# Turning keys by VectorE in 32x32 squares instead of by TensorE, in a two-layer encoder step

## The chip, the cores and the metric

The kernel runs on one core of one Trainium2 chip. The metric is the device time of one execution in microseconds; lower is better. TensorE (PE) multiplies, VectorE (DVE), ScalarE (ACT) and GpSimd (POOL) work on elements, SyncE (SP) issues nearly all DMA transfers, ACT issues a few, and sixteen DMA engines carry them out.

## The reference

A streaming encoder step with two groups, a prompt of 2048 frames and a sample of 64 frames that follow 2048 cached ones. Layer a is attention over a band of chunks, layer b is stick-breaking attention over all earlier frames. 16 heads of 64, width 1024, all in float32. Besides the two results it returns the new keys and values:

```python
qp, kp, vp, gp = a_project(xp, norm_a[i], w_in_a[i])        # layer a: rms_norm, then one product
op = chunk_band_prompt(qp, kp, vp, rel_bias_a[i])
k_all = jnp.concatenate([cache_a_k[i], ks], axis=1)         # 512 cached rows, then 64 new ones
o_s = band_attend(qs, k_all, v_all, q_pos_s, k_pos_a, rel_bias_a[i])
xp = xp + gated_out(op, gp, w_out_a[i])
...
kb_p, vb_p = shared_kv(xp, norm_kv, w_kv)                   # layer b
kb_all = jnp.concatenate([cache_b_k, kb_s], axis=1)         # 2048 cached rows, then 64 new ones
op = sb_prompt(qp, kb_p, vb_p)
o_s = sb_block(qs, kb_all, vb_all, q_pos_s, k_pos_b)
...
return (y_prompt, y_sample, new_a_k_prompt, new_a_v_prompt, kb_p, vb_p,
        new_a_k_sample, new_a_v_sample, kb_s, vb_s)
```

Keys enter as rows of one frame (`cache_a_k`, `cache_b_k`: frames x 1024) and leave as rows of one frame (`new_a_k_prompt`: the last 512 frames of the prompt, `kb_p`: all 2048, and the two of the sample). Inside, the kernel keeps keys with the features on the partitions and the frames along the row. So keys are turned on the way in and on the way out.

## The kernel before

The program goes through four stages: projections of layer a (to about 656 us in the profile), band attention of layer a (to about 1300 us), projections of layer b (to about 2030 us) and stick-breaking attention of layer b. Products are made in split form: each operand is held as a high and a low part, and three products are added.

`projections` first makes the values, then runs jobs: for layer a the kinds k, q, g, for layer b k, g, q, each over eight pairs of heads (`hp`). A job loads 128 columns of weights (`wraw`, on ACT's DMA queue), splits them, multiplies them with the turned inputs (`x_own` for the first 1088 frames, `big` for the other 1024) into banks of PSUM (`ps_t`, five buffers), and empties each bank: ACT copies the high part (`sh`), DVE subtracts for the low part (`sl`); `g` jobs have one part, `sg`. These tiles have five buffers and are stored to scratch memory by SP. For some kinds (`DEFER`) the second half is left for later jobs that run beside the attention. Of layer a's keys the second half is such a job; of layer b's keys nothing is.

Between the jobs stand pieces of staging, shared out evenly by program order. Those that the change touches, or that it stands beside:

- `stage_cache` (from L430) takes 512 cached frames of one pair of heads: it loads `kr` (L434, 512 rows of 512 bytes, one buffer), turns it by four PE transposes into the PSUM bank `ps_c`, splits that into `kh` and `kl` and stores both. Layer a has 8 such pieces, layer b 32, of which 8 are staged in layer a's projections and 24 in layer b's.
- `stage_diff` (`vcur`, `vprev`) makes differences of values, and `stage_w_out` (`vcur` from `w_out_b`, stored to `wo`) splits the last weights; they have no turns, but share queues and buffers.
- `natural` (from L509) writes keys' rows for the outputs: `kf` is the sum of high and low part (made by POOL), four PE transposes turn it into the bank `ps_n`, ACT copies it to `kn` (two buffers), and one DMA stores it (L515). In layer b it runs for four blocks of 512 frames of each pair, in both layers for the 64 frames of the sample.
- `token_rows`, in the late jobs, does the same for the last 512 frames of layer a's prompt: `lkn` into `ps_r`, a copy by ACT, a store through `queue`.

The banks `ps_c`, `ps_n` and `ps_r` come from one pool of three (`bank`, tag `wt`), which other transposes and late jobs use too.

Each engine and each DMA queue works in order. Within the projections the order is set by a scheduler that simulates the program; within the attention stages instructions keep program order, except some loads and stores. At the end of layer b's projections stand `LEAD["b"] = 14` steps of late jobs on PE (six products of 512 columns each) before the first scores; the first loads of the attention (`q`, `kt`, `vt`) come behind `gf`, the last norm's weights, on SP's queue.

```python
def flip(out, in_):
    pe.transpose(out, in_, ident[: in_.shape[0], : in_.shape[0]])
...
staged += [partial(stage_diff, "cache", t, i) for t in range(PAST // P) for i in range(2)]
keys_b = [partial(stage_cache, "b", hp, c) for hp in range(HP) for c in range(PAST // CH)]
staged += keys_b[:8]
```

Of the kernel before, what the change touches and what calls it, by code (L numbers as in the profile page):

```python
# [9 lines left out]
F32 = mybir.dt.float32  # L10
F32R = mybir.dt.float32r
AF = mybir.ActivationFunctionType
# [4 lines left out]
P = 128  # L17
# [15 lines left out]
CH = 512  # L33
# [32 lines left out]
def place(r):  # L66
    h, c = spot(r)
    return HALVES[h][0] + c


def f32(ap):
    return ap.bitcast(F32)
# [28 lines left out]
def encoder_step(ctx: ExitStack, tc: tile.TileContext, a: dict, o: dict):  # L101
    nc = tc.nc
    order = InOrder(tc)
    dve, act, gps, pe = (order.engine(x) for x in (nc.vector, nc.scalar, nc.gpsimd, nc.tensor))
    mm = pe.matmul

    def in_place(what):


        def pinned():  # L110
            was, order.on = order.on, order.amid
            what()
            order.on = was

        return pinned
# [23 lines left out]
    queue = Queue(24)  # L139
# [13 lines left out]
    def bank(name):  # L153
        return turned_ps.tile([P, CH], F32, name=name, tag="wt", bufs=3)
# [17 lines left out]
    for L, rows in (("a", CACHE_A), ("b", PAST)):  # L172
# [3 lines left out]
            q=[dram.tile([3, P, T], F32R, name=f"q_{L}{i}") for i in range(HP)],  # L176
# [24 lines left out]

    def flip(out, in_):
        pe.transpose(out, in_, ident[: in_.shape[0], : in_.shape[0]])

    banks, ends = {}, {}
    done_late = set()
# [2 lines left out]
    def split(hi, lo, src):  # L209
        act.activation(hi, src, AF.Copy)  # L210
        dve.tensor_tensor(lo, src, f32(hi), ALU.subtract)

    def scaled_split(hi, lo, src, g):
        for k in range(src.shape[1]):
            act.activation(hi[:, k], src[:, k], AF.Copy, scale=g[:, k : k + 1])
            dve.scalar_tensor_tensor(lo[:, k], src[:, k], g[:, k : k + 1], f32(hi[:, k]), ALU.mult, ALU.subtract)
# [16 lines left out]
    def put(L, kind, hp, s, cols, part, by=nc.sync.dma_start):  # L233

        for i in (0, 2) if kind == "q" and s == 0 else (s,):
            by(f32(lay[L][kind][hp][i, :, cols]), f32(part))


    def projections(L, x_of, begin, w_v, cv, gv, out_v, jobs, first, prompt, sample, stages):
        with (  # L240
# [7 lines left out]
            with tc.tile_pool(name=f"v_{L}", bufs=2) as pool:  # L248
# [12 lines left out]
                def turned(t, scale=gps.tensor_scalar, xt=None):  # L261
                    r0, n = TOK[t]
                    if xt is None:
                        xt = normed(t, scale)
                    halves = []
                    for k0 in range(0, NK, 4):
                        ps = bank("ps_tr").rearrange("p (k t) -> p k t", k=4)
                        for k in range(4):
                            flip(ps[:, k, :n], xt[:n, (k0 + k) * P : (k0 + k + 1) * P])
                        halves.append(ps[:, :, :n])  # L270
                    return halves
# [158 lines left out]
    def stage_cache(L, hp, c, pool):  # L430
        rows, cols = slice(c * CH, c * CH + CH), slice(hp * P, hp * P + P)
        to = slice(T + c * CH, T + c * CH + CH)
        kr = pool.tile([P, 4, P], F32, name="kr", tag="kr", bufs=1)
        nc.sync.dma_start(kr, a[f"cache_{L}_k"][rows, cols].rearrange("(j p) c -> p j c", p=P))  # L434
        ps = bank("ps_c")
        for j in range(4):
            flip(ps[:, j * P : j * P + P], kr[:, j])
        kh = pool.tile([P, CH], F32R, name="kh", tag="kh", bufs=1)
        kl = pool.tile([P, CH], F32R, name="kl", tag="kl", bufs=1)
        split(kh, kl, ps)  # L440
        for s, part in enumerate((kh, kl)):
            put(L, "k", hp, s, to, part)
        if L == "b":
            return
        vr = pool.tile([P, 4, 2, DH], F32, name="vr", tag="vr", bufs=2)
        nc.sync.dma_start(
            vr.rearrange("p j h d -> p j (h d)"), a[f"cache_{L}_v"][rows, cols].rearrange("(j p) c -> p j c", p=P)
        )
        vs = pool.tile([P, 4, 2, P], F32R, name="vs", tag="vs", bufs=2)
        for h in range(2):  # L450
            split(vs[:, :, h, :DH], vs[:, :, h, DH:], vr[:, :, h])
        nc.sync.dma_start(
            f32(lay[L]["v"][to, 2 * hp : 2 * hp + 2]).rearrange("(j p) h c -> p j h c", p=P), f32(vs)
        )
# [52 lines left out]


    def natural(pool, kf, at, n, nt, dst):  # L509
        ps = bank("ps_n").rearrange("p (j c) -> p j c", j=4)  # L510
        for j in range(nt):
            flip(ps[:n, j], kf[:, at + j * n : at + j * n + n])
        kn = pool.tile([P, 4, P], F32, name="kn", tag="kn", bufs=2)
        act.activation(kn[:n, :nt], ps[:n, :nt], AF.Copy)
        nc.sync.dma_start(dst.rearrange("(j p) c -> p j c", p=n), kn[:n, :nt])  # L515


    def there(L, kind, hp, r):
# [217 lines left out]
    def late_job(L, kind, w, c0, g, hp, x2, first, prompt):  # L736
        st = {}

        def load():
            if L not in KEPT:  # L740
                st["raw"] = opool.tile([P, NK, P], F32, name="lraw", tag="og", bufs=1)
                c = c0 + hp * P
                sp.dma_start(st["raw"], w[:, c : c + P].rearrange("(k p) c -> p k c", p=P))
            st["wh"] = opool.tile([P, NK, P], F32R, name="lwh", tag="oh", bufs=2)
            st["wl"] = opool.tile([P, NK, P], F32R, name="lwl", tag="ol", bufs=2)
            if L in KEPT:
                for i, part in enumerate((st["wh"], st["wl"])):
                    sp.dma_start(f32(part), f32(lay[L]["w"][kind, hp][i]))

        def cut(k0):  # L750
            ks = slice(k0, k0 + STEP)
            scaled_split(st["wh"][:, ks], st["wl"][:, ks], st["raw"][:, ks], g[:, ks])

        def some(c, k0):
            if k0 == 0:
                st["ps"] = bank("ps_j")
            ps, wh, wl = st["ps"], st["wh"], st["wl"]
            cols = slice(c, c + CH)
            for k in range(k0, k0 + STEP):
                mm(ps, wh[:, k], x2[0][:, k, cols], start=(k == 0), stop=False)  # L760
                mm(ps, wh[:, k], x2[1][:, k, cols], start=False, stop=False)
                mm(ps, wl[:, k], x2[0][:, k, cols], start=False, stop=(k == NK - 1))

        def out(c):
            ps = st["ps"]
            at = slice(place(HALF + c), place(HALF + c) + CH)
            if kind == "g":
                sg = opool.tile([P, CH], F32, name="sg", tag="xr", bufs=2)
                act.activation(sg, ps, AF.Sigmoid)
                dve.tensor_tensor(sg, ps, sg, ALU.mult)  # L770
                queue.store(lay[L]["g"][hp][:, at], sg)
            else:
                sp = opool.tile([P, 2, CH], F32R, name="sp", tag="xr", bufs=2)
                split(sp[:, 0], sp[:, 1], ps)
                for s in range(2):
                    put(L, kind, hp, s, at, sp[:, s], queue.store)
                st[c] = sp
            if c + CH == HALF:
                done_late.add((L, kind, hp))

        def add_back(c):

            st["kn"] = opool.tile([P, 2, CH], F32, name="lkn", tag="xr", bufs=2)
            gps.tensor_tensor(st["kn"][:, 0], f32(st[c][:, 0]), f32(st[c][:, 1]), ALU.add)

        def token_rows(c):
            kn = st["kn"]
            ps = bank("ps_r")
            for j in range(4):
                flip(ps[:, j * P : j * P + P], kn[:, 0, j * P : j * P + P])  # L790
            act.activation(kn[:, 1], ps, AF.Copy)
            b = HALF + c - first
            dst = prompt[b : b + CH, hp * P : hp * P + P]
            queue.store(dst.rearrange("(j p) c -> p j c", p=P), kn[:, 1].rearrange("p (j c) -> p j c", j=4))

        chunks = range(0, HALF, CH)
        behind = []
        for c in chunks:
            rows = kind == "k" and HALF + c >= first
            behind.append([partial(out, c)] + ([(2, partial(add_back, c)), (4, partial(token_rows, c))] if rows else []))  # L800
        products = [partial(some, c, k0) for c in chunks for k0 in range(0, NK, STEP)]
        cuts = [] if L in KEPT else [partial(cut, k0) for k0 in range(0, NK, STEP)]
        return [in_place(x) for x in [load] + cuts], products, behind
# [257 lines left out]
    staged[0] = first_stage  # L1061
# [3 lines that stand above are left out]
    staged_b = []  # L1065
# [197 lines left out]
    with (  # L1263
# [13 lines left out]
        for h in range(2):  # L1277
            rows = slice(h * DH, h * DH + DH)
# [267 lines left out]
```

## Time and profile before

| what | before |
|---|---|
| timed runs | 3275.82, 3279.91 (the median), 3280.48 us |
| span of the profiled execution | 3278.2 us |
| instructions | 53687 |
| DMA packets | 464892, 688.41 MB, mean 210 GB/s |
| share of SP's queue / ACT's queue of 16 engines | 61.8% / 4.8% |

The profile gives no other time of its execution than the span, which lies between the lowest and the median of the timed runs. The page shows busy time of each engine, the span in 40 equal slices as tenths of busy time, and the chain of work that ended last. The view by windows repeats the busy times for chosen stretches; the view of one tile lists the instructions that write or read it, with the shortest, median and longest duration in ns; the view of DMA gives packets, MB and the share of sixteen engines for each queue (q1 is SP's, q10 ACT's). PE is TensorE's matmul, PEld its weight load.

### The profile page before, as it was taken

The page shows a single profiled execution, that of the slowest core. Times are in us where ns is not written, and L with a number is a line of the kernel's source. Part 1 is how long each engine was busy: PE and PEld are TensorE (multiplying, and loading weights), DVE is VectorE, ACT ScalarE, POOL GpSimd, SP SyncE. Part 2 cuts the span into 40 slices and gives each one's busy share as a digit, 9 for nine tenths or more (in the row PEclk, how much of TensorE's full clock was granted, in tenths as well). Part 3 has the DMA queues.
Part 4 walks back from the last instruction along what each step waited for, and adds up shares of the span by engine and source line. Part 5 has one row for each costly group of instructions (what it writes and reads, how often), then busy time and mean ns, then how long its engine had stood idle before and what let it go on. Part 6 is the DMA issues. An engine that isn't in the chain of part 4 may idle for free.

```text
span 3278.2 us, 53687 instructions
## 1 busy us (share of the span) xinstructions
PE 3204.2 (98%) x17928; PEld 2791.0 (85%) x17928; DVE 1887.0 (58%) x3786; ACT 1711.4 (52%) x3719; POOL 1291.4 (39%) x1950
## 2 busy tenths in 40 slices
PE   8999999999998999999999999999999989999999
PEld 7889999988887898878889998788888878888877
DVE  4235431147778775231044333788878878888873
ACT  5234222258888776143134442566666656666662
POOL 3001110026665554020044200444477766877761
PEclk9999999999999999999999999999999999999999
DMA  6359993387899983553399999977735566455423
GB/s 202 121 185 368 349 331 118 117 237 220 240 260 267 252 237 130 164 174 128 113 357 352 348 357 328 251 217 217 213 121 148 162 203 174 124 143 141 138 72 119
DMA packets 464892, 688.41 MB, mean 210 GB/s; under 512 B 51446, under 2 KB 261398, under 8 KB 464615
## 3 DMA queue, kind: packets, MB, share of 16 engines
q1 hardware_dynamic: 405158, 633.85, 61.8%
q10 hardware_dynamic: 59456, 51.13, 4.8%
q8 instruction: 143, 2.34, 0.3%
q14 instruction: 135, 1.10, 0.1%
HBM read 408.78 MB, written 276.07 MB: 209 GB/s over the span
## 4 chain that ended last, share of the span: by engine, by line
PE 75%; issue 7%; DVE 6%; DMA 6%; ACT 2%; POOL 2%; SPq 1%; POOLq 0%; ACTq 0%; DVEq 0%
PE ps_t L90 23%; PE ps_v L90 11%; PE acc L90 10%; PE z L90 9%; PE wt L90 8%; PE ps_j L90 6%; PE ps_o L90 5%; DVE s L90 3%; DVE pl L90 2%; DMA vt<-v_b 1%; PE ps_tr L90 1%; ACT ph L90 1%; DMA kt<-k_b 1%; POOL s L90 1%; ACT s L90 1%
## 5 line engine op out<-in xcount | busy, mean ns | idle before, releaser
L90 DVE TENSOR_TENSOR pl<-wt,ph 128x512 fp32r<-128x512 f32 (+1 forms) x864 | 551.9, 654 | 122.4 <-ACT ph L90 118.7
L90 ACT ACTIVATE ph<-wt 128x512 fp32r<-128x512 f32 (+1 forms) x864 | 485.7, 578 | 205.4 <-PE wt L90 178.2
L90 PE MATMUL ps_t<-x_own,wh 128*128 128x362 f32 (+1 forms) x2304 | 567.5, 327 | 0.0
L90 PE MATMUL wt<-ident,s 128*128 128x128 f32 x3472 | 551.5, 274 | 13.4 <-DVE pl L90 6.8
L90 PEld LDWEIGHTS wt<-ident,s 128*128 128x128 f32 x3472 | 418.6, 141 | 88.3 <-DVE pl L90 12.9
L90 ACT ACTIVATE f<-z 128x512 f32<-128x512 f32 (+4 forms) x680 | 355.1, 535 | 196.1 <-PE z L90 139.7
L90 PEld LDWEIGHTS ps_t<-x_own,wh 128*128 128x128 f32 x2304 | 405.0, 188 | 1.8
L90 POOL TENSOR_TENSOR s<-f,s 128x256 f32<-128x256 f32 x416 | 361.3, 870 | 104.2 <-DVE s L90 95.9
L90 PE MATMUL acc<-ph,vt 128*128 128x512 f32 (+3 forms) x1088 | 376.2, 381 | 14.1 <-DMA vt<-v_b 7.5
L90 PE MATMUL z<-kt,q 128*128 128x512 f32 (+3 forms) x1280 | 375.4, 381 | 12.9 <-DMA q<-q_b 5.8
L90 PE MATMUL ps_t<-x_own,wl 128*128 128x362 f32 (+1 forms) x1152 | 376.7, 327 | 0.0
L90 PE MATMUL acc<-pl,vt 128*128 128x512 f32 (+3 forms) x1088 | 364.6, 368 | 7.2 <-DVE pl L90 6.8
L90 POOL TENSOR_SCALAR s<-s,rc 128x640 f32<-128x640 f32 (+5 forms) x264 | 199.2, 760 | 387.3 <-DMA keys<-k_a 193.3
L90 PE MATMUL ps_o<-big,oh 128*128 128x512 f32 x1088 | 336.2, 392 | 0.2 <-ACT oh L90 0.2
L90 POOL TENSOR_TENSOR two<-f 128x256 f32<-128x256 f32 x416 | 259.5, 626 | 166.3 <-ACT f L90 150.0
L90 DVE TENSOR_TENSOR_SCAN s<-two,s,own 128x256 f32<-128x256 f32 x408 | 299.7, 738 | 33.6 <-POOL two L90 32.3
L90 PEld LDWEIGHTS z<-kt,q 128*128 128x128 f32 x1280 | 221.9, 192 | 43.5 <-ACT f L90 11.8
L90 PE MATMUL ps_j<-big,lwh 128*128 128x512 f32 x768 | 246.9, 397 | 1.1 <-DVE pl L90 0.6
L90 PE MATMUL ps_t<-big,wh 128*128 128x512 f32 x768 | 238.9, 391 | 0.0
L90 PEld LDWEIGHTS ps_o<-big,oh 128*128 128x128 f32 x1088 | 202.2, 188 | 41.3 <-ACT oh L90 0.4
L90 PEld LDWEIGHTS acc<-ph,vt 128*128 128x128 f32 x1088 | 198.7, 192 | 37.1 <-ACT ot L90 8.4
L90 DVE CUSTOM_DVE_ANT_0 s<-z,bias 128x640 f32<-128x640 f32 (+4 forms) x256 | 184.7, 733 | 77.2 <-PE wt L90 51.1
(148 smaller groups left out, 5528.9 us busy)
## 6 DMA issues: line engine op xcount, KB each, us to landing
vt<-v_b SPq DMA_DIRECT2D x80, 512.0 KB, 4.9
v_b<-vs SPq DMA_DIRECT2D x64, 512.0 KB, 5.7
q<-q_a SPq DMA_DIRECT2D x128, 256.0 KB, 5.9
q<-q_b SPq DMA_DIRECT2D x128, 256.0 KB, 4.6
vt<-v_a SPq DMA_DIRECT2D x48, 512.0 KB, 7.1
kt<-k_b SPq DMA_DIRECT2D x96, 256.0 KB, 5.6
keys<-k_a SPq DMA_DIRECT2D x80, 256.0 KB, 7.1
v_a<-vs ACTq DMA_DIRECT2D x32, 512.0 KB, 2.7
```

What stands on the lines that cost most here:

```text
L90: ins = op(*args, **kwargs)
```

## The change

The 32x32 turn on VectorE turns each square of a tile by itself, so a tile of 128 x 512 comes out with every square turned and left in its place. To finish the job, the squares have to change places, and the transfers do this: four DMAs, one for each block `q` of 32 columns of the rows, move 32 x 16 x 32 elements, in pieces of 32 elements (128 bytes). For the cached keys the squares are placed by the load and then turned; for the outputs they are turned and then placed by the store.

```diff
+    Q = 32
+
+    def by_squares(rows):
+
+        return [rows[:, q * Q : q * Q + Q].rearrange("(i b) a -> b i a", b=Q) for q in range(P // Q)]
+
+    def squares_of(tile_, n):
+        return [tile_[q * Q : q * Q + Q, :n].rearrange("b (i a) -> b i a", a=Q) for q in range(P // Q)]
...
-        kr = pool.tile([P, 4, P], F32, name="kr", tag="kr", bufs=1)
-        nc.sync.dma_start(kr, a[f"cache_{L}_k"][rows, cols].rearrange("(j p) c -> p j c", p=P))
-        ps = bank("ps_c")
-        for j in range(4):
-            flip(ps[:, j * P : j * P + P], kr[:, j])
+        kr = pool.tile([P, CH], F32, name="kr", tag="kr", bufs=1)
+        for to_, of in zip(squares_of(kr, CH), by_squares(a[f"cache_{L}_k"][rows, cols])):
+            nc.sync.dma_start(to_, of)
+        ps = pool.tile([P, CH], F32, name="kc", tag="kc", bufs=1)
+        dve.transpose(ps, kr)
...
     def natural(pool, kf, at, n, nt, dst):
-        ps = bank("ps_n").rearrange("p (j c) -> p j c", j=4)
-        for j in range(nt):
-            flip(ps[:n, j], kf[:, at + j * n : at + j * n + n])
-        kn = pool.tile([P, 4, P], F32, name="kn", tag="kn", bufs=2)
-        act.activation(kn[:n, :nt], ps[:n, :nt], AF.Copy)
-        nc.sync.dma_start(dst.rearrange("(j p) c -> p j c", p=n), kn[:n, :nt])
+        m = n * nt
+        kn = pool.tile([P, CH], F32, name="kn", tag="kn", bufs=2)
+        dve.transpose(kn[:, :m], kf[:, at : at + m])
+        for to, of in zip(by_squares(dst), squares_of(kn, m)):
+            nc.sync.dma_start(to, of)
...
         def token_rows(c):
             kn = st["kn"]
-            ps = bank("ps_r")
-            for j in range(4):
-                flip(ps[:, j * P : j * P + P], kn[:, 0, j * P : j * P + P])
-            act.activation(kn[:, 1], ps, AF.Copy)
+            dve.transpose(kn[:, 1], kn[:, 0])
...
-            queue.store(dst.rearrange("(j p) c -> p j c", p=P), kn[:, 1].rearrange("p (j c) -> p j c", j=4))
+            for to, of in zip(by_squares(dst), squares_of(kn[:, 1], CH)):
+                queue.store(to, of)
```

The first place is PE in layer b's projections, between the k jobs of two pairs of heads, before the change. `ps_t` is a bank of products, `big` and `x_own` are the turned inputs, `wh` and `wl` the weights, `kr` and `kf` what is turned:

```order
L90 MATMUL ps_t<-big_15803,wl 128x512
L90 MATMUL ps_c<-ident,kr 128x128 x4
L90 MATMUL ps_n<-ident,kf 128x128 x8
L90 MATMUL ps_t<-big_15803,wh 128x512
L90 MATMUL ps_t<-big_15804,wh 128x512
L90 MATMUL ps_t<-big_15803,wl 128x512
L90 MATMUL ps_t<-x_own_15801,wh 128x364
```

After the change no row with `ps_c`, `ps_n` or `ps_r` is left on PE; the products stand without them.

The second place is SP between the k jobs of the second and third pair of layer b, before the change:

```order
L236 DMA k_b_120<-sl 128x1024
L472 DMA vcur<-v_raw 128x512
L483 DMA v_b<-vs 128x1024
L474 DMA vprev<-v_raw 128x512
L472 DMA vcur<-v_raw 128x512
L515 DMA out_b_k_s<-kn 64x128
L483 DMA v_b<-vs 128x1024
L474 DMA vprev<-v_raw 128x512
L515 DMA out_b_k_p<-kn 128x4x128
L434 DMA kr<-in_cache_b_k 128x4x128
L236 DMA k_b_122<-kh 128x512
L236 DMA k_b_122<-kl 128x512
```

And the same place with the change:

```order
L245 DMA k_b_120<-sh 128x1024
L444 DMA kr<-in_cache_b_k 32x16x32
L245 DMA k_b_120<-sl 128x1024
L444 DMA kr<-in_cache_b_k 32x16x32
L245 DMA k_b_121<-kh 128x512
L444 DMA kr<-in_cache_b_k 32x16x32
L245 DMA k_b_121<-kl 128x512
L523 DMA out_b_k_p<-kn 32x16x32 x4
L523 DMA out_b_k_s<-kn 32x2x32 x4
L481 DMA vcur<-v_raw 128x512
```

Each load of `kr` and each store of `kn` is now four issues, and they stand among the stores of the jobs' results.

The third place is the end of layer b's projections on SP, from the last store of q to the first load of the attention, before the change:

```order
L236 DMA q_b_118<-sl 128x1088
L90 DMA lwh<-w_bq_149 128x1024
L90 DMA lwl<-w_bq_149 128x1024
L236 DMA k_b_126<-kh 128x512
L236 DMA k_b_126<-kl 128x512
L127 DMA gate_b_128<-sg 128x512
L1313 DMA gf<-in_norm_f 128x1024
L134 DMA q<-q_b_111 64x2x512 x2
```

With the change the last rows of the same stretch are these:

```order
L127 DMA q_b_111<-sp 128x512 x5
L501 DMA wo_165<-vs 256x1x512
L498 DMA vcur<-in_w_out_b 128x512
L501 DMA wo_165<-vs 256x1x512
L498 DMA vcur<-in_w_out_b 128x512
L501 DMA wo_166<-vs 256x1x512 x2
L1319 DMA gf<-in_norm_f 128x1024
L134 DMA q<-q_b_111 64x2x512 x2
```

Pieces of `stage_w_out` and of the cached keys, which stood among the jobs before, now stand behind the last store of q and ahead of `gf`. In layer a's projections the eight pieces of layer b's cached keys moved the other way, from among the g jobs to among the q jobs.

## The prediction, made before the changed kernel ran

> **What bounds the kernel now.** I read the page first, then the busy time by stage, then the DMA traffic of the stages in which the changed lines run.
>
> ```profile
> PE 3204.2 (98%) x17928; PEld 2791.0 (85%) x17928; DVE 1887.0 (58%) x3786; ACT 1711.4 (52%) x3719; POOL 1291.4 (39%) x1950
> ...
> DMA  6359993387899983553399999977735566455423
> ...
> PE 75%; issue 7%; DVE 6%; DMA 6%; ACT 2%; POOL 2%; SPq 1%; POOLq 0%; ACTq 0%; DVEq 0%
> ```
>
> TensorE is busy for 98% of the span and carries most of the chain that ended last, so work taken off it should shorten the run. But the row of DMA shows two stretches of nines while keys are projected: slices 4 to 6 (layer a) and 21 to 26 (layer b). The view by windows gives, behind each window, the busy time of PE, PEld, DVE, ACT and POOL, the granted clock, the DMA share and GB/s:
>
> ```profile
> 246.00:328.00 82.00, 82.00 (x507) 81.19 (x506) 43.94 (x120) 34.57 (x96) 11.09 (x13) 1.00 1.03 368
> 410.00:492.00 82.00, 82.00 (x434) 74.74 (x433) 28.14 (x56) 23.16 (x55) 15.64 (x12) 1.00 0.93 331
> 492.00:574.00 82.00, 82.00 (x445) 75.85 (x444) 12.60 (x35) 21.55 (x54) 2.59 (x2) 1.00 0.33 117
> ...
> 1638.00:1842.00 204.00, 202.96 (x1147) 185.35 (x1146) 87.51 (x152) 82.01 (x189) 83.15 (x68) 1.00 0.99 352
> 1842.00:1936.00 94.00, 94.00 (x586) 93.80 (x585) 32.57 (x79) 40.34 (x107) 3.92 (x3) 1.00 0.99 341
> 1936.00:2032.00 96.00, 95.82 (x576) 93.05 (x575) 34.09 (x85) 31.80 (x82) 0.37 (x1) 1.00 0.96 359
> ```
>
> From 1638 to 2032 us (layer b: jobs k, then g, then q) PE is full, and the DMA engines are full too: 0.99, 0.99 and 0.96. Two resources are balanced there, and the change takes from one and gives to the other. In layer a the nines are followed by a quiet stretch (0.33 from 492 us).
>
> **What the change takes away.** Turns of keys on PE:
>
> ```profile
> L90 PE MATMUL ps_c<-ident,kr x160: 270/272/330, 225.7 to 2019.1; 128*128 128x128 f32 x160
> ...
> L90 PE MATMUL ps_n<-ident,kf x144: 270/272/329, 236.1 to 1850.3; 128*128 128x128 f32 x128, 128*64 128x128 f32 x16
> L90 ACT ACTIVATE kn<-ps_n x48: 252/591/605, 236.4 to 1870.0; 128x512 f32<-128x512 f32 x32, 64x128 f32<-64x128 f32 x16
> ...
> L90 PE MATMUL ps_r<-ident,lkn x32: 270/272/328, 716.5 to 1007.1; 128*128 128x128 f32 x32
> ```
>
> 160 + 144 + 32 = 336 transposes go, with 48 + 8 copies on ACT. A transpose lasts 272 ns but overlaps its neighbours, so its price is read from the times at which things start:
>
> ```profile
> 1791.87 0.62 PE L90 MATMUL ps_t<-big,wh 128*128 128x512 f32 x2
> ...
> 1792.33 0.39 PE L90 MATMUL ps_t<-big,wl 128*128 128x512 f32 x1
> ...
> 1792.56 0.60 PE L90 MATMUL ps_c<-ident,kr 128*128 128x128 f32 x4
> ...
> 1792.91 0.71 PE L90 MATMUL ps_t<-big,wh 128*128 128x512 f32 x2
> ...
> 1793.46 0.40 PE L90 MATMUL ps_t<-big,wl 128*128 128x512 f32 x1
> ```
>
> Two 512-column products take 1792.33 - 1791.87 = 0.46 us; from 1792.56 to 1793.46, 0.90 us, stand four transposes and two such products. So four transposes cost 0.44 us, one 0.11. In all 336 x 0.11 = **37 us of PE**: layer a's projections hold 16 groups of four (8 cached keys of a, 8 of b) and 8 singles, 7.9 us; the late jobs of layer a 8 groups, 3.5 us; layer b's projections 24 + 32 groups and 8 singles, 25.5 us.
>
> **What it adds.** On DVE 40 + 48 + 8 = 96 turns (88 of 128x512, 8 of 128x64). No row shows this operation; the nearest are
>
> ```profile
> L90 DVE TENSOR_TENSOR kl<-ps_c,kh x40: 676/692/693, 232.6 to 2020.1; 128x512 fp32r<-128x512 f32 x40
> ...
> L90 DVE SCALAR_TENSOR_TENSOR vwl<-vraw,g_kv,vwh x16: 741/748/1620, 1409.8 to 1532.3; 128x512 fp32r<-128x512 f32 x16
> ```
>
> so I bound one by 0 and 1.62 us and take 0.69. Layer b's projections then hold 56 x 0.69 = 39 us more on DVE (at most 91), beside 154 us busy of 394: hidden by the matmuls. If that cover went, the 39 us would show. But a turn into kn now waits on DVE for the stores that still read that buffer, and the subtractions that empty the matmul banks (sl) queue behind it.
>
> The dearer part is in the DMA. Each transfer of 512 rows x 128 columns (256 KB) is 512 packets of 512 bytes now and becomes four transfers with 2048 packets of 128 bytes together. No 128-byte packet is in the trace; the neighbours, as packets, MB and share of 16 engines, are (windows 492 to 656 us, 13.8 to 14.9 us, 2494.4 to 2497.2 us):
>
> ```profile
> q10 hardware_dynamic: 5200, 2.62, 5.8%
> ...
> q1 hardware_dynamic: 1738, 0.05, 97.4%
> ...
> q1 hardware_dynamic: 292, 0.07, 11.2%
> ```
>
> The first is nearly all 512-byte packets: 0.058 x 164 x 16 / 5200 = 29 ns each. The second is nearly all 4-byte packets: 0.974 x 1.1 x 16 / 1738 = 9.9 ns. In the third, 256 packets of 256 bytes (a 32 KB store and a 32 KB load) and about 35 tiny ones take 0.112 x 2.8 x 16 = 5.0 us; less 0.3 for the tiny ones, 18 ns each. From 9.9 to 29 ns the cost rises about evenly with size, so I estimate **13.5 ns** for 128 bytes, bounds 9 and 18. A transfer of 256 KB goes from 512 x 29 = 14.8 to 2048 x 13.5 = 27.6 us of one engine: 0.80 us of all sixteen, 0.83 with the packets that signal its three more ends. In layer b's projections 32 + 24 such transfers make 46 us, and the eight small ones 1: **+47 us** (bounds 16 and 78).
>
> The Trainium skill ("DMA: Bandwidth & Descriptors", Specifications) says that line rate needs 512 bytes and that below it the engine reads, modifies and writes. The 256-byte row, half of it stores to HBM, shows no such surcharge at 18 ns; no run here shows 128 bytes.
>
> Last, SP issues three more DMAs per transfer:
>
> ```profile
> L515 SPq DMA_DIRECT2D out_b_k_p<-kn x32: 388/530/1482, 1647.1 to 1870.6; - x32
> ...
> L434 SPq DMA_DIRECT2D kr<-in_cache_b_k x32: 383/384/1392, 321.0 to 2014.9; - x32
> ...
> L134 SPq DMA_DIRECT2D q<-q_b x128: 573/597/1306, 2031.7 to 3105.6; - x128
> ```
>
> One issue costs 0.38 to 0.60 us. By the order of SP, 369 issues stand between the last v output of layer b and gf; now 570. At 0.58 these are 331 us, under the DMA engines' own time below, so I charge SP nothing as long as it may run while the engines drain. What hides it is the DMA backlog; without that cover the 201 issues show.
>
> **The sum.** Layer b from 1638 to 2032: DMA busy 0.99 x 204 + 0.99 x 94 + 0.96 x 96 = 387 us; plus 47 is 434. PE needs 394 - 25 = 369. So DMA becomes the bound, and the stretch lasts 434 us at full engines instead of 394: **+40**. It can't be made up behind it: the order puts 37 issues instead of 8 between the last q store and gf, and the first loads of layer b's attention (q, kt, vt) stand behind gf on SP's queue; PE has only its fourteen lead steps to cover them. The 25.5 us saved on PE there become idle time. In layer a the shift is 8 x 0.83 = 7 us, and eight cached keys of b move from the g jobs into the q jobs; the quiet stretch takes up what is late, so I credit the 7.9 us on PE in full. The late jobs give 3.5, and cost 7 us of DMA in a stage at 0.77 to 0.97, which I leave at nothing.
>
> +40 - 7.9 - 3.5 = +28.6 on the profiled span of 3278.2 gives 3306.8. The span is 1.7 us under the median of the timed runs (3279.91), so the same step from the median gives 3308.5. I say **3308**.
>
> **Rivals.** *Hidden transfers, faster.* Part of the 387 us is waiting inside packets, which does not grow with small ones; if the engines have 47 us of air, all 37 us come off PE: 3243 from the median, or 3255 with some 12 us for the longer tail ahead of gf. For it: PE shows no idle time at 0.99. Against it: 1.03 is the highest share quoted above, and 1.03 x 394 - 387 leaves 19 us of air. It decides below that; packets at the lower bound of 9 ns add 16 us, and then, with engines at 1.00, 387 + 16 - 394 - 11.4 gives 3277.5, no change.
>
> *SP is the bound, slower still.* SP waits in order for producers (1600 to 2000 us: total, times, longest):
>
> ```profile
> SPq L434 <- PE ps_c L90: 24.7, 8, 5.4
> SPq L361 <- ACT vn L90: 22.5, 5, 5.2
> ```
>
> If such waits stay while 201 issues join at 0.38 to 0.58 us, the stretch grows by 76 to 117 us: 3345 to 3386, decided where issuing plus waiting exceeds 434 us. Against it: a late queue finds its producers done, and the largest wait, on ps_c, goes with the transposes.
>
> *Small stores cost double.* 32 x 2048 stores at another 13.5 ns are 55 us more: 3364. That is also what the skill's rule on 512 bytes would give.
>
> *The cover is missing in the wrong place.* If DVE holds up sl behind a full kn, PE stalls inside the jobs as well; bounded by DMA again, it stays within the main case's upper half.
>
> That the change would not do what it says is excluded by the order of PE: no turn into ps_c, ps_n or ps_r is left.
>
> **How the numbers follow.** Main case, DMA the bound in layer b's projections: 0.62, 3285 to 3340 (12 ns with engines at 1.03, to 18 ns with engines at 1.00). Hidden, faster: 0.14. No change (packets near 9 ns): 0.08. SP the bound: 0.09. Double stores: 0.07. The range from 3265 to 3360 leaves out most of the hidden case and the upper part of the last two. A measurement of this kernel tells about 0.2%, 6.6 us, from no change. Faster 0.14, same 0.09, slower 0.77.
>
> **What would show it.** The stretch from the first k store of layer b to the first load of q should last about 434 us instead of 394, with the DMA share at 1.0 and PE busy well below it, some 65 us idle; 128-byte packets near 13.5 ns; the band and the attention stages as long as before; layer a's projections about 8 us shorter. I am wrong if PE stays full from 1638 us on (transfers hidden), if the DMA share falls while the stretch grows (SP, or waits on DVE), or if the transposes' 0.11 us do not come off in layer a.

## The result

| | before | after |
|---|---|---|
| median of the timed runs | 3278.03 us (4 runs, 3275.82 to 3280.48) | 3337.26 us (4 runs, 3334.60 to 3339.35) |
| span of the profiled execution | 3278.2 us | 3334.5 us |
| DMA packets | 464892 | 595450 |

The ratio is 1.0179, 95% interval [1.0166, 1.0191]: the change makes the kernel 59 us slower. The forecast was 3308 us, 30 us slower. Its reason holds; the stretch that it priced grew by more than its sum, and its credit from layer a was not paid.

The page of the changed kernel, with the rows that answer to those of before (busy time; PE and DMA in 40 slices; the chain that ended last):

```profile
PE 3179.4 (95%) x17592; PEld 2766.3 (83%) x17592; DVE 1925.0 (58%) x3882; ACT 1684.6 (51%) x3663; POOL 1291.2 (39%) x1950
...
PE   8999999999998999999987899699999999999999
...
DMA  6359996288899883453599999987745556455423
...
PE 68%; DMA 10%; issue 7%; DVE 7%; SPq 3%; ACT 3%; POOL 1%; ACTq 0%; POOLq 0%; DVEq 0%
```

PE has 25 us less work (3204.2 before) and yet the run is longer: in slices 21 to 23 and in slice 26 (layer b's projections and the way into its attention) PE falls to 8, 7, 8 and 6 tenths. DMA's share of the chain rises from 6 to 10%, SP's from 1 to 3%. The view by windows (columns as in the prediction: PE, PEld, DVE, ACT, POOL, clock, DMA share, GB/s) places it:

```profile
1638.00:1842.00 204.00, 171.31 (x845) 154.93 (x844) 84.56 (x162) 51.00 (x124) 60.36 (x51) 0.92 0.97 283
1842.00:1936.00 94.00, 79.68 (x439) 78.12 (x438) 36.20 (x80) 30.99 (x81) 21.82 (x18) 0.91 0.98 292
1936.00:2032.00 96.00, 96.00 (x594) 96.00 (x593) 39.28 (x100) 37.69 (x102) 2.87 (x3) 1.00 1.04 353
1638.00:2098.00 460.00, 393.14 (x2118) 370.06 (x2116) 179.39 (x376) 136.63 (x339) 85.05 (x71) 0.93 0.98 308
```

PE is idle for 33 us of the first window, where it was full; the DMA engines stay at 0.97 to 1.04. In the first two windows TensorE's granted clock is 0.92 and 0.91, where it was 1.00, so a part of PE's busy time there is work at a lower clock (over the run the mean product of `x_own` and `wh` takes 331 ns instead of 327). The same points of the program, by the time at which they start in the two traces:

| point of the program | before, us | after, us | shift |
|---|---|---|---|
| first load of q, layer a's attention | 668.6 | 661.1 | -7.6 |
| score product of layer a, 1001 us before | 1001 | 993 | -8.5 |
| score product of layer a, 1033 us before | 1033 | 1033 | -0.5 |
| first store of k, layer b | 1638.5 | 1641.9 | +3.4 |
| first store of gate, layer b | 1841.2 | 1880.1 | +38.9 |
| last issue of q's low part, layer b | 2020.0 | 2057.2 | +37.2 |
| first load of q, layer b's attention | 2031.7 | 2098.3 | +66.6 |
| score products of layer b, from 2110 us before | 2110 | 2168 | +57.7 |
| last product of the outputs (ps_o) | 3270.5 | 3326.8 | +56.3 |

Three things happen. Layer a's projections gain the 7.6 us, the gain is lost again near 1010 us, and from the first k store to the first load of layer b's attention the program takes 456 us instead of 393.

What PE waits for most from 1600 to 2110 us (total, times, longest), before the change:

```profile
PE z L90 <- DMA q<-q_b: 5.8, 2, 3.6
```

and after it, with what DVE's turns wait for (one row of the tile kn: total, times):

```profile
PE ps_t L90 <- DVE sl L90: 40.0, 8, 11.1
PE z L90 <- DMA vt<-v_b: 28.9, 1, 28.9
```

```profile
  DMA out_b_k_p<-kn: 28.5, 13
```

The row with `sl` is rival four's mechanism: the turn into kn waits for a buffer that its stores still read, and sl, which empties the matmul banks, queues behind it. The row with `vt` is the boundary: PE has done its lead and waits 28.9 us for layer b's first loads. The end of SP's queue before them (start, duration, instruction):

```profile
2085.70 0.62 SPq L498 DMA_DIRECT2D vcur<-in_w_out_b  x1
2087.72 0.53 SPq L501 DMA_DIRECT2D wo<-vs  x1
2088.29 0.60 SPq L498 DMA_DIRECT2D vcur<-in_w_out_b  x1
2092.91 2.41 SPq L501 DMA_DIRECT2D wo<-vs  x2
2097.93 0.33 SPq L1319 DMA_DIRECT2D gf<-in_norm_f  x1
2098.32 1.30 SPq L134 DMA_DIRECT2D q<-q_b  x2
```

Staging that is late stands ahead of gf, and at the very end SP stands still for 4.0 and 2.6 us (2088.89 to 2092.91, 2095.32 to 2097.93) around the last stores of `wo`.

### The profile page after: what moved, and what is told of

It reads as the page before. It is cut to its first block, busy times and chain, and to the rows that moved or that the text cites. A ratio compares the mean times of both kernels' runs of the same rounds, so it can differ in the third digit from the quotient of the medians.

```text
span 3334.5 us, 53349 instructions
## 1 busy us (share of the span) xinstructions
PE 3179.4 (95%) x17592; PEld 2766.3 (83%) x17592; DVE 1925.0 (58%) x3882; ACT 1684.6 (51%) x3663; POOL 1291.2 (39%) x1950
## 2 busy tenths in 40 slices
DMA packets 595450, 688.40 MB, mean 206 GB/s; under 512 B 223989, under 2 KB 391957, under 8 KB 595174
## 4 chain that ended last, share of the span: by engine, by line
PE 68%; DMA 10%; issue 7%; DVE 7%; SPq 3%; ACT 3%; POOL 1%; ACTq 0%; POOLq 0%; DVEq 0%
PE ps_t L90 17%; PE ps_v L90 11%; PE acc L90 10%; PE z L90 9%; PE wt L90 8%; PE ps_j L90 6%; PE ps_o L90 5%; DVE s L90 2%; DVE pl L90 2%; DMA vt<-v_b 1%; SPq L523 1%; PE ps_tr L90 1%; DMA vprev<-v_raw 1%; DVE wl L90 1%; DMA keys<-k_a 1%
## 5 line engine op out<-in xcount | busy, mean ns | idle before, releaser
L90 PEld LDWEIGHTS ps_t<-x_own,wh 128*128 128x128 f32 x2304 | 412.9, 192 | 46.3 <-issue 18.2
L90 PE MATMUL z<-kt,q 128*128 128x512 f32 (+3 forms) x1280 | 376.8, 382 | 35.6 <-DMA vt<-v_b 28.9
L90 PEld LDWEIGHTS acc<-pl,vt 128*128 128x128 f32 x1088 | 194.8, 190 | 40.3 <-DVE pl L90 25.2
```

Of the source, the lines that this page charges most:

```text
L90: ins = op(*args, **kwargs)
```

## The bill of the DMA engines in layer b's projections

From the first store of k to the first load of q of layer b's attention, all packets of the trace, by size: how many, their mean duration, and the sum as time of sixteen engines.

```
bytes        before                     after               difference
    4    5764   9.0 ns    3.2 us     8852   9.0 ns    5.0 us     +1.8
  128       0                      112640  12.9 ns   91.0 us    +91.0
  512   49671  27.7 ns   85.9 us    20480  29.3 ns   37.5 us    -48.4
 2048   20096  89.7 ns  112.6 us    21059  93.9 ns  123.5 us    +10.9
 4096   10880 169.4 ns  115.2 us    11004 175.0 ns  120.3 us     +5.1
 4352    6144 175.6 ns   67.4 us     6144 178.4 ns   68.5 us     +1.1
all sizes               386 us                      447 us     +61
```

The cut into 128-byte pieces and the signals of more transfers cost 91.0 - 48.4 + 1.8 = 44 us: the term of the prediction was 47. The other 17 us it did not have. At the durations of before, the changed counts of the large sizes (late jobs' loads and stores that the order now puts ahead of gf) are worth 963 x 89.7 + 124 x 169.4 ns over sixteen engines, 6.7 us. The rest, 10.4 us, is that each large packet takes 2 to 5% longer. The small pieces are not shown to be the cause of that: in run 5 below, whose stretch holds no 128-byte packet, the 2048-byte packets take 94.8 ns and those of 4352 bytes 182.9. Both stretches run at 0.98: 386/393 and 447/456.

## The experiments

Three theories. **D**: the engines' time sets layer b's stretch. **S**: SP's queue does, by issuing and by waiting in order. **V**: DVE's turns do, behind full buffers. Each run is compared with the kernel before on the same chip. The diffs are against the kernel named.

**1 to 3. The change by parts** (against the changed kernel: in runs 1 and 2 two of its three parts are put back, in run 3 one).

```diff
# cached keys only: natural and token_rows as before
-        dve.transpose(kn[:, :m], kf[:, at : at + m])
+            flip(ps[:n, j], kf[:, at + j * n : at + j * n + n])
# outputs only: stage_cache and token_rows as before
-        dve.transpose(ps, kr)
+            flip(ps[:, j * P : j * P + P], kr[:, j])
# no late rows: token_rows as before
-            dve.transpose(kn[:, 1], kn[:, 0])
+                flip(ps[:, j * P : j * P + P], kn[:, 0, j * P : j * P + P])
```

> Only the cached keys are turned by squares; output rows stay with PE and ACT. Three theories on what sets the length of layer b's projections with the change: D, the DMA engines' time for 128-byte packets; S, SP's issues; V, the wait of VectorE for the stores that still read kn, which holds up the subtractions behind it. D: 24 transfers in layer b's stretch cost 24 x 0.83 = 20 us of DMA, so the stretch grows by 15 to 25 us; 3290 to 3303. S: 72 more issues, a third of the 201, so a third of the loss (22 of 67 us at the first load of q): much the same, 3295 to 3305. V: no kn is turned by VectorE, so little is lost: 3270 to 3283.

> Only the rows for the outputs of the projections are turned by squares; cached keys and the late rows stay with PE. D: 32 transfers and 8 small ones, 27 us of DMA: the stretch grows by 22 to 35 us, 3298 to 3313. V: all of the loss is here, 3325 to 3340. S: 120 issues, 60% of the loss, 3310 to 3320. The sum of this loss and that of the run before should be about the 59 us of the change under D and S.

> The change without its third part: the late jobs' rows of layer a's prompt stay with PE, ACT and one store of 512-byte pieces. The 8 us that layer a's projections win are lost again near 1000 us, where a store of o_a takes 9 us to land. If a DMA peak of its own stands there (weights of w_out_a, values, keys), it is there without the late rows too: 3333 to 3342, and the lead over the kernel before is gone after 1040 us. If the small stores of the late rows make the peak, the lead of 8 us lives on: 3326 to 3331.

Measured: cached keys only 3296.88 us, ratio 1.0058 [1.0041, 1.0075]; outputs only 3318.51, 1.0119 [1.0103, 1.0134]; without the late rows 3331.26, 1.016 [1.0144, 1.0175], 6 us under the full change. The first two add up to 56 of 59 us. Cached keys only lies in the ranges of D and of S, so it doesn't tell them apart. With cached keys alone PE ends its products of layer b 15.2 us earlier than before, and the first load of q comes 20.3 us later all the same, with the engines full over the stretch (window from the first k store to that load):

```profile
1635.00:2052.00 417.00, 390.86 (x2245) 370.17 (x2243) 170.66 (x337) 153.65 (x377) 84.47 (x70) 0.98 0.99 339
```

So there the loss lies wholly in the queue ahead of gf, not in PE's stalls. The outputs came out 5 us above D's range and inside S's (3310 to 3320). The third run answers where layer a's gain went. PE in 1000 to 1020 us, before, after and without the late rows' small stores, in this order:

```profile
1000.00:1020.00 20.00, 15.29 (x105) 13.02 (x104) 16.78 (x42) 16.06 (x38) 10.14 (x11) 1.00 1.04 313
```

```profile
1000.00:1020.00 20.00, 8.75 (x63) 7.73 (x60) 11.69 (x29) 8.21 (x18) 2.88 (x5) 0.87 1.07 268
```

```profile
1000.00:1020.00 20.00, 12.69 (x75) 11.14 (x74) 12.30 (x30) 12.05 (x27) 6.50 (x9) 0.83 0.87 253
```

In the changed kernel PE does 8.8 us of work in these 20, at a DMA share of 1.07. The chain that ended last runs there through a store (start, duration):

```profile
1011.76 9.27 DMA o_a<-ot
...
1021.11 0.60 ACT ot L90
...
1021.76 3.71 PE acc L90 x12
```

Before the change the chain runs through the same store, and it takes about as long:

```profile
1009.88 8.91 DMA o_a<-ot
```

So the store is not slower; SP issues it late. Its issue on SP, before, after and without the late rows' part, in this order:

```profile
1009.88 1.10 SPq L127 DMA_DIRECT2D o_a<-ot  x1
```

```profile
1011.76 0.32 SPq L127 DMA_DIRECT2D o_a<-ot  x1
```

```profile
1001.43 1.49 SPq L127 DMA_DIRECT2D o_a<-ot  x1
```

The tile that it stores was finished (by POOL, `ot<-ot,gt`) at 1008.8, 998.8 and 996.7 us. So the store stands in SP's queue for 1.1, 12.9 and 4.8 us, and PE's lead is used up while it stands there. At the score product that starts at 1010.9 us before, PE leads by 12.0 us in the changed kernel and by 12.1 without the late rows' part; at the one that starts at 1070.7 us the lead is 0.1 and 7.6. So some 4.5 us are lost at this peak in any case, and what else is lost goes with the late rows' small stores.

**4. Turns without small transfers** (against the changed kernel). Each of the 128x512 transfers is one DMA of 512-byte pieces again, DVE turns stay. The squares are not placed, so cached keys and the outputs' keys are not the reference's; the work of every engine is.

```diff
-        for to_, of in zip(squares_of(kr, CH), by_squares(a[f"cache_{L}_k"][rows, cols])):
-            nc.sync.dma_start(to_, of)
+        nc.sync.dma_start(
+            kr.rearrange("p (j c) -> p j c", j=4), a[f"cache_{L}_k"][rows, cols].rearrange("(j p) c -> p j c", p=P)
+        )
```

> VectorE turns the squares as in the change, but the transfers stay as before: one DMA with 512-byte pieces for each load and store of four blocks (the squares are not moved to their places, so keys and key rows are not the reference's). PE is relieved of its 37 us, the DMA has nothing more. D: layer b's stretch is still bounded by the DMA's 387 us, so it shortens by 7 to 18 us and not by 25; layer a's gain is lost near 1000 us: 3258 to 3272. If PE alone were the bound: 3241 to 3248. V: VectorE still waits for kn, and the loss stays: 3300 or more.

Measured: 3269.38 us, ratio 0.9972 [0.9961, 0.9982], a gain of 10 us, D's value. PE's products of layer b end 28.1 us earlier than before, and the first load of q comes at the same time as before (2031.7 us):

```profile
PE z L90 <- DMA vt<-v_b: 28.1, 1, 28.1
PE ps_t L90 <- DVE sl L90: 4.4, 1, 4.4
```

```profile
1631.00:2032.00 401.00, 376.24 (x2125) 356.86 (x2123) 180.82 (x381) 137.84 (x340) 87.37 (x72) 0.98 0.98 353
```

All that PE saves in layer b it waits for vt at the boundary, at a DMA share of 0.98. So the engines, not PE, would have set this stretch even with almost nothing cut smaller (only the stores of 64 frames still are). And the wait on sl is 4.4 instead of 40.0 us with the same turns on DVE: V is not a cause, it follows from late stores.

**5 and 6. More issues, then smaller pieces, with TensorE's turns** (against the kernel before).

```diff
-        nc.sync.dma_start(kr, a[f"cache_{L}_k"][rows, cols].rearrange("(j p) c -> p j c", p=P))
+        src = a[f"cache_{L}_k"][rows, cols].rearrange("(j p) c -> p j c", p=P)
+        for j in range(4):                       # run 5: pieces of 512 bytes
+            nc.sync.dma_start(kr[:, j], src[:, j])
+        for q in range(0, P, 32):                # run 6 instead: pieces of 128 bytes
+            nc.sync.dma_start(kr[:, :, q : q + 32], src[:, :, q : q + 32])
```

The stores of kn are cut in the same way.

> The kernel before, with TensorE's turns as they were, but each load of kr and each store of kn issued as four DMAs whose pieces stay 512 bytes (192 issues more in all). If the DMA engines' time is what the change costs (D): only the signals of the extra ends are added, about 3 us of sixteen engines: 3276 to 3288 us. If it is SP's issuing (S): 192 issues at about 0.58 us with PE's work unrelieved: 3325 us or more, and the DMA share between 1638 us and gf falls below 0.95.

> As the run before (four issues each, TensorE turns), but the four DMAs cut the rows into pieces of 128 bytes; same count of issues, same PE work, only the pieces differ. D: 47 us more DMA in layer b's projections on top of engines that are full: 3325 to 3350 us, with the DMA share at 0.96 to 1.0 and the start of layer b's attention some 50 to 65 us late. S: the same time as the run before within 5 us. V (DVE's turn waiting for kn, and the matmul banks behind it): no turn on DVE is left, so a loss of under 10 us.

Measured: four issues of 512-byte pieces 3331.31 us, ratio 1.0163 [1.0147, 1.0178]; with 128-byte pieces 3358.90, 1.0247 [1.0232, 1.0262]. The first is a plain miss of D and a hit of S: 53 us, without one byte of data more. Of these, 16.5 us are there at the first k store already (10 at the first load of layer a's attention); the stretch grows by 44 us. Its windows and PE's waits from 1600 to 2110 us:

```profile
1638.00:1842.00 204.00, 186.66 (x1004) 165.32 (x1003) 70.20 (x128) 68.20 (x164) 67.55 (x57) 0.97 0.83 277
1655.00:2093.00 438.00, 408.67 (x2315) 381.03 (x2314) 147.59 (x315) 151.78 (x377) 85.63 (x72) 0.98 0.90 315
```

```profile
PE ps_n L90 <- POOL kf L90: 13.4, 9, 2.4
PE ps_c L90 <- DMA kr<-in_cache_b_k: 8.6, 6, 2.9
```

The engines are at 0.83 in the k jobs: not full. PE stands in its own order before turns whose input is late. SP issues 528 transfers in this stretch (341 before), 320 us of the 438, and stands between issues in the rest. We read this as SP's queue needing about 438 us by itself when it has some 190 issues more; the time that PE loses in its own order is not told apart from it. The second run adds 28 us. That is above D's range (3325 to 3350) and not S's "within 5 us": most of the 441 us of engine work runs beside what SP needs anyway.

**9 and 10. Which of the two binds the changed kernel** (against it). Run 9 keeps every issue and leaves three quarters of `kb_p` unwritten (that output alone, contrary to what the expectation says of layer a); run 10 keeps every packet and moves the issues of kr from SP to ACT's queue.

```diff
         for to, of in zip(by_squares(dst), squares_of(kn, m)):
-            nc.sync.dma_start(to, of)
+            nc.sync.dma_start(to[:part], of[:part])      # run 9: part = 8 of 32
...
-            nc.sync.dma_start(to_, of)
+            nc.scalar.dma_start(to_, of)                 # run 10
```

> The changed kernel with all its issues and turns, but each of the four stores of kn for the prompt writes only 8 of its 32 rows of squares (three quarters of kb_p and of new_a_k_prompt's early rows are left unwritten): 512 instead of 2048 packets per transfer. In layer b this takes 32 x 1536 x 13.0 ns = 40 us of sixteen engines away and no issue. D (the engines' time binds): 3295 to 3312 us, the first load of q of layer b 25 to 40 us earlier than in the changed kernel. S (SP's issues bind): 3330 to 3342 us, unchanged. If each is nearly as late as the other: between, a gain of 10 to 25 us.

> The changed kernel, but the four loads of kr are issued by ACT on its own queue: the same packets, 96 issues fewer on SP in layer b's projections (56 us at 0.58), 96 more on ACT, which is busy for under half of that stretch. D: 3328 to 3345 us, unchanged. S: 3285 to 3312 us, with the DMA share above that of the changed kernel. If each is nearly as late as the other: a gain of 5 to 15 us.

Measured: 3312.33 us, ratio 1.0105 [1.009, 1.012] for run 9, a gain of 25 us on the changed kernel; 3334.93, 1.0174 [1.0158, 1.0189] for run 10, 2 us, no change. One window of each, from its first k store to its first load of q:

```profile
1637.00:2072.00 435.00, 380.22 (x2101) 358.55 (x2099) 177.95 (x372) 133.62 (x337) 83.73 (x68) 0.93 0.93 308
```

```profile
1641.00:2092.00 451.00, 387.26 (x2109) 364.40 (x2107) 179.96 (x379) 135.02 (x339) 82.95 (x70) 0.94 0.97 311
```

With 42 us less engine work (405.6 instead of 447.2) the stretch shrinks by 20 us, to 436, and the engines are no longer full: 0.93. What is left is not PE's time, since at the boundary PE waits longer in run 9 than in the changed kernel:

```profile
PE z L90 <- DMA vt<-v_b: 37.0, 1, 37.0
```

With 89 issues fewer on SP the engines are about as full as in the changed kernel, 0.97, and the stretch shrinks by 5 us. Run 10 is not pure: kr now stands in ACT's order, and ACT held up its copies for it:

```profile
ACT sh L90 <- DMA kr<-in_cache_b_k: 31.7, 5, 9.2
```

The runs in one table (first k store to first load of q; engine work as the sum of all packets' time over sixteen; SP's issues in that stretch):

```
run                               stretch   engine work   share   SP issues
before                             393 us     386 us       0.98      341
turns only (4)                     401        394          0.98      375
cached keys only (1)               417        411          0.99      415
outputs only (2)                   439        429          0.98      472
a quarter of the stores' bytes (9) 436        406          0.93      533
many issues, PE turns (5)          438        396          0.91      528
kr issued by ACT (10)              451        440          0.98      444
after                              456        447          0.98      533
small pieces, PE turns (6)         464        441          0.95      533
```

Two limits lie close together. Where the share is 0.98 or more, the stretch is the engine work divided by 0.98, to 2 us. Where some 530 issues go through SP with light transfers (runs 5 and 9), it is 436 to 438 us; run 1, with slightly more engine work than run 9 but 415 issues, takes 417. In the changed kernel the engines' limit, 447/0.98 = 456, is the higher one; the one that we read as SP's lies 20 us under it. Run 6 fits neither: at 0.98 its engine work would take 450 us, and it takes 464.

**7, 8, 11 and 12. Moving the cached keys of layer b into layer a's quiet stretch.** Run 7 does it to the changed kernel, run 8 to the kernel before, runs 11 and 12 to run 1 (cached keys by DVE, everything else by TensorE), with 24 and with all 32 pieces in layer a.

```diff
-    staged += keys_b[:8]
+    staged += keys_b[:24]                                # run 12: all 32
...
-        staged_b += [partial(stage_diff, "new", t, half), *keys_b[8 + i : 9 + i]]
+        staged_b += [partial(stage_diff, "new", t, half), *keys_b[24 + i : 25 + i]]
```

> The changed kernel, but 24 instead of 8 of layer b's 32 pieces of cached keys are staged in layer a's projections, where the DMA share after 492 us was 0.48. Sixteen pieces at (27.6 + 21.5)/16 = 3.07 us leave the full stretch of layer b, 49 us. D: 3280 to 3298 us, layer b's attention starting some 45 us earlier than in the changed kernel, layer a's projections up to 5 us longer. S: 16 pieces are 16 x 6 issues, 56 us at 0.58, so about the same gain: D and S are not told apart by this run, but by it against the next. V: at most 10 us gain, since 32 turns into kn stay.

> Control: the same move of sixteen pieces in the kernel before. D: 36 us of DMA leave layer b, but PE is full there and only 7 us of transposes move from one stage to the other, so no change: 3272 to 3284 us; the start of layer b's attention stays within 10 us. If layer b's stretch was bounded by DMA before the change already (as the turn-only run, which freed PE and gained nothing there, lets one think): with PE at 394 us full it still cannot gain more than 7 us there.

> Only the cached keys are turned by DVE (outputs and late rows by TensorE as before), and 24 of layer b's 32 pieces are staged in layer a. D: the 8 pieces left in layer b add 7 us of DMA there while 16 pieces (49 us) have left it, so TensorE binds again, 160 transposes shorter (17.6 us) less some 5 lost near 1000 us: 3260 to 3275 us, faster than both kernels. S: 8 x 3 issues more and 16 x 6 fewer than with cached keys alone: the same range. If layer a's projections can't take the pieces: 3280 us or more.

> As the run before with all 32 pieces in layer a: no cached key is left in layer b's projections. Layer a's quiet stretch takes 25 us more of DMA (it had 164 x 0.52 = 85 us free in the changed kernel, less 49 for the 16 pieces): 3258 to 3275 us if it fits, 5 to 15 us worse than the run before if the tail runs into layer a's attention.

| run | us | ratio, interval |
|---|---|---|
| 7, the changed kernel, 24 in a | 3288.86 | 1.0031 [1.0017, 1.0045] |
| 8, the kernel before, 24 in a | 3272.89 | 0.9982 [0.9973, 0.9992] |
| 11, cached keys only, 24 in a | **3253.71** | **0.9926 [0.9911, 0.9941]** |
| 12, cached keys only, 32 in a | 3270.04 | 0.9972 [0.9962, 0.9982] |

Of the 48 us that run 7 gains on the changed kernel, 42 are in layer b's stretch (414 us instead of 456), from which 48 us of engine work have gone (447 to 399); the first k store comes 8 us earlier too. Run 8 gains little, 5.8 us: with 349 us of engine work in 373 us, TensorE binds, and it has lost only 7 us of transposes there. Run 11 joins both: less engine work in layer b and fewer transposes. Of its 25 us, 6 come with the move alone (run 8); the other 19 are near the price of 160 transposes, 17.6 us. Its layer a, 492 to 656 us, and its layer b stretch:

```profile
492.00:656.00 164.00, 164.00 (x878) 150.73 (x877) 53.85 (x113) 54.48 (x131) 14.76 (x11) 1.00 0.73 231
1630.00:2000.00 370.00, 368.84 (x2154) 351.86 (x2153) 144.37 (x304) 142.37 (x358) 86.98 (x71) 1.00 0.96 335
```

PE stays full in both, and a share of 0.48 in the changed kernel's quiet stretch has become 0.73. It is the one version that beats both kernels clearly, 6 us below its expected range. Run 12 goes too far: the pieces run past layer a's projections (the last load of kr is at 683 us), its attention begins 22 us later than before, and PE stands still for longer at its start, in 656 to 720 us (its busy time there is 59 us before the change):

```profile
656.00:720.00 64.00, 50.35 (x232) 42.31 (x231) 25.33 (x67) 23.30 (x56) 6.91 (x9) 0.84 0.81 228
```

## Why the prediction came out as it did

- **What binds** (DMA in layer b's projections, the boundary behind it): right. The share is 0.98 over the stretch, and the first loads are late behind gf. Run 9 shows it by taking bytes away, run 4 shows the boundary without the small pieces. PE was to be idle some 65 us there and is for 460 - 393 = 67, but that agreement is luck: the window is 26 us longer than the 434 of the sum, and PE is busy for 393 us instead of 369, at a mean granted clock of 0.93 where it was 1.00.
- **PE's saving of 37 us**: right where it can be seen. Layer a's projections end 7.6 us earlier (7.9 foretold). In run 4, where little else holds PE up, its lead of 5.3 us at layer b's values has grown to 28.1 at the last product of q: 22.8 us, after 5.9 us of waits on sl and wh, against 25.5.
- **DVE's turn, 0.69 us by its neighbour**: right. The row of the tile kc:

```profile
L90 DVE STREAM_TRANSPOSE kc<-kr x40: 662/704/712, 225.7 to 2071.0; 128x512 f32<-128x512 f32 x40
```

- **The 128-byte packet, 13.5 ns**: right, 12.9 in this stretch and 13.0 over all 167936. The rival of double-priced stores falls: with cached keys only (run 1) all 128-byte packets belong to loads, and they take 13.0 ns; with the outputs only (run 2) all belong to stores, and they take 12.9. The Trainium skill ("DMA: Bandwidth & Descriptors", Specifications) has transfers below 512 bytes read, modified and written; that this doubles a store's time was the prediction's reading. In cost per byte 128-byte pieces are dearer by 4 x 12.9 / 27.7 = 1.9, but nothing in these runs sets stores apart from loads.
- **The stretch, +40 us** ("387 plus 47 is 434, at full engines"): right in its mechanism, mis-sized, it measured +63. The 47 were 44. Missing were 6.7 us of transfers that the order moved ahead of gf (whose 37 issues the prediction counted, but not their time on the engines), 10.4 us of longer large packets, and the engines ran at 0.98 where the sum took 1.00, which is worth 9 us (447/0.98 - 447).
- **SP charged nothing**: right for this kernel, by runs 9 and 10, but with little room: if the 436 to 438 us of runs 5 and 9 are SP's own limit, it lies 2 to 4 above the predicted 434. The prediction's price for SP (a stretch of 470 to 511 us) was too high, since its waits shrink as its queue gets late: gaps between its issues are 160 us before and 78 after.
- **Layer a's 7.9 and the late rows' 3.5 us, credited in full**: wrong, the credit was 0. The lead was there, 12.0 us at 1010.9 us, and gone at 1033. The late rows' 7 us of DMA, "which I leave at nothing", fell on a peak where the engines are at 1.04 to 1.07. There a store of `o_a` that PE's next products hang on stood in SP's queue for 12.9 us (4.8 without the late rows' part, 1.1 before), so that PE, though 12 us ahead, went on no earlier than before. The 0.77 to 0.97 that the prediction went by are means over slices of 82 us; the peak is 20 us long.
- **"It can't be made up behind it"**: about 10 us were (+66.6 at the first load of q, +56.3 at the end). From the first score to the first sum of values the changed kernel takes 9.1 us (2108.1 to 2117.3), the one before 14.1; that the lead's transfers, now ahead of gf, no longer share the engines with the first loads would explain it, but no run tests this.

Together: +40 - 7.9 - 3.5 = +28.6 was forecast. Measured in the profile: 3.4 at the first k store, 63 in the stretch, -10 behind it, +56.3. That the time lies inside the main case's 3285 to 3340 is in part luck: the upper end of that range stood for packets of 18 ns, the packets took 12.9, and terms that the sum did not have filled the room.

What stays open: whether SP's limit in runs 5 and 9 is the time to issue or its waits in order (it issues for 72 to 73% of that stretch and stands the rest); what sets run 6's stretch, 14 us over the higher of the two limits; and why large packets take longer in some runs than in others. DVE's turns with four issues of 512-byte pieces were not tried.

## What to carry to other kernels

Taking work from an engine that is 98% busy buys next to nothing in a stage where the DMA engines are 98% busy too: look for the stage's second full resource first, and ask what stands ahead of the next stage's first load. Price small packets per packet, from neighbours in the trace, and then add what the longer queue moves ahead of the boundary. Work that loads a full stage may be free in another one a few hundred microseconds earlier: one number in the staging (8 to 24) was worth 43 us here with the cached keys turned by DVE (run 1 to run 11), though only 6 us in the kernel before (run 8).

## What the runs showed of the hardware

- A packet's time goes nearly with its size above a small fixed part: 9.0 ns for 4 bytes, 27.7 for 512, 89.7 for 2048, 169.4 for 4096 in layer b's stretch before the change, 12.9 for 128 after it. Large ones vary from run to run by some per cent (2048 bytes: 89.7 ns before, 93.9 after, 94.8 in run 5). Loads and stores of 128 bytes cost the same (13.0 in run 1, 12.9 in run 2).
- How long SP takes to issue a DMA depends on what else is queued. The four stores of kn took a median of 564 ns per issue in the changed kernel and 326 ns when they carried a quarter of the bytes; the loads of layer b's kr, which are the same in both, took 651 and 502. The row of the lighter stores, shortest, median and longest:

```profile
L524 SPq DMA_DIRECT2D out_b_k_p<-kn x128: 277/326/1214, 1629.8 to 1885.3; - x128
```

So an SP that issues for 87% of the k jobs, as in the changed kernel (207 of 238 us), is no proof that SP is the limit: with nearly as many issues there (305 against 320) and lighter transfers it is 76%, and the k jobs take 204 us.
